# Mixture-of-experts stage: tokens gathered as one f32 product instead of three bfloat16 parts, scratch tiles shared, a twentieth slot in the weight ring

## The chip, the cores and the metric

The kernel runs on one core of a Trainium2 chip. The metric is the device time in microseconds (us) of one execution, lower is better; comparisons use the median of several runs. Five engines work side by side, each through its own queue in order: TensorE (PE in the profile; PEld is its weight load), VectorE (DVE), ScalarE (ACT), GpSimd (POOL) and SyncE (SP), which here issues the DMAs.

## The reference

One layer over 256 tokens of 1024 channels in f32. A modulated norm feeds a Fourier branch and a two-way state-space scan; their gated sum goes through an output projection to the residual `x`. The change lies in the second half:

```python
h2 = rmsnorm(x, norm2_w) * (1.0 + sc2) + sh2
x = x + g2 * moe_ffn(h2, w_router, b_router, w_gate_up, b_gate_up, w_down, b_down)
return rmsnorm(x, final_norm_w)

# moe_ffn, for each of 256 tokens: the 4 best of 32 experts, softmax over the 4 logits
gu = xe @ w_gate_up[e] + b_gate_up[e]            # 1024 -> 2048
gate = minimum(gu[:, :1024], 7.0)
up = clip(gu[:, 1024:], -7.0, 7.0)
act = (up + 1.0) * gate * sigmoid(1.702 * gate)
y = act @ w_down[e] + b_down[e]                  # weighted and added to its token
```

## The kernel before

Everything up to about 560 us (input product, scan, Fourier branch, output projection) is left alone by the change. From there the kernel computes the norm and the routing, and then 32 experts one after the other.

**Weights.** Each expert has 12 chunks of 1 MB: eight of gate/up (one for each 128 of the 1024 input channels) and four of down. `expert_chunk` (L984) issues them on SP's queue, in order, into a ring of tiles: 8 slots `a0` to `a7` in pool `ringA`, 11 slots `b0` to `b10` in `ringB`, 19 in all, taken in the order of the list `RING`. Slots that hold other things in the earlier stage (`xr`, `gn`, `sn2`, `few`, or memory of the earlier stage's tiles under `ringB`) come late in that list. A chunk is issued when its slot's last reader is done and when fewer than 8 are in flight; SP does this in order, so one that waits holds up all behind it. Expert e+1's chunks stand ahead of expert e's work in the program, so about one and a half experts are in the ring.

**The branch of each expert.** An expert's first 64 tokens are always computed. More of them are handled in `overflow(e)`, a chain of branches `tc.If(n_e > 64)` (L1425), `n_e > 96` (L1427) and `n_e > 128` (L1429) which every engine takes, SP too. SP can issue no chunk beyond `If(e)` before PE has come to it, and the slots of e's gate chunks are given back there. `block32` (L1386 to L1408) computes 32 more tokens. In the profiled execution experts 9, 20 and 24 run it once each; I call that a spill.

**Tokens of an expert.** `normed(tb)` (L1097) makes the normed tokens `h2` of one half (128 of 256 tokens) in place, in f32, on DVE. `high_part` (ACT, L1132) and `low_part` (POOL or DVE, L1135) split them into three bfloat16 tiles `h2p[tb][0..2]` whose sum is the f32 value; `h2p` is the first half's tiles and `h2q` the second's. `choose` (L1117 to L1122) picks the four experts, `ranks` numbers the tokens of each expert, and `one_hot` (L1184) writes 0/1 matrices `oh`. `gather_tokens` (L1189) multiplies a token tile with `oh`, so the chosen tokens come out as columns: for each of 8 channel groups k and both halves tb three bfloat16 products, summed in PSUM. One call of `gather` (k4 = 0 or 1) does four of the groups, 24 products. A pair of experts shares one gather of 128 columns; expert e does half of the gather of the next pair (`gather(xe[1 - p2], oh[1 - p2], e % 2)`, for e from 2 to 29), expert 1 does two halves, and `first_gather` does the first pair's. In `block32` the gather has 32 columns and all 16 (k, tb) pairs, 48 products.

**Order within an expert.** PE, DVE, ACT and POOL follow the written order (`manual_schedule`): gate_up (L1277, bias L1287), gather, in even experts `scatter_pair(0)` (L1332), the transposes of `act_T` (L1316), in even experts `scatter_pair(1)`, the branch, down (L1323). Meanwhile DVE and ACT make the activation `ga`, `up` (L1292 to L1297) and `aT`.

Of the kernel before, what the change touches and what calls it, by code (L numbers as in the profile page):

```python
# [9 lines left out]
F32 = mybir.dt.float32  # L10
F32R = mybir.dt.float32r
BF16 = mybir.dt.bfloat16
I32 = mybir.dt.int32
AF = mybir.ActivationFunctionType
# [9 lines left out]
ALPHA = 1.702  # L24
LIMIT = 7.0
CAP = 64
NRA, NRB = 8, 11
PAD = 80

MOD_RATE = {"fourier": 1.0, "gates": 0.5, "z": 0.9}  # L30

# [30 lines left out]
def build(tc, A, out):  # L62
    nc = tc.nc
    V, S, G, T = nc.vector, nc.scalar, nc.gpsimd, nc.tensor
# [20 lines left out]
    ident = ctab[:, C_ID:C_ID + 128]  # L85
# [219 lines left out]
    for k in range(8):  # L305
# [3 lines left out]
        ps = bank("y", 1) if k % 4 == 3 else bank("mm", 3)  # L309
# [119 lines left out]
    for j in range(4):  # L429
        i = j // 2  # L430
        for m, (col, N) in enumerate(FIRST):
# [5 lines left out]
            for k in (2 * j, 2 * j + 1):  # L437
                kw = dict(start=m % 2 == 1, skip_group_check=True) if N == 256 else {}
# [177 lines left out]
    w = next_w()  # L616
    for g in (2, 3):
        with ExitStack() as es:
            if g == 2:
                es.enter_context(tc.issue_after(made.ins))  # L620
            ps = project(w, g, 512)
# [3 lines left out]
    w = next_w()  # L625
# [328 lines left out]
    ms = ExitStack()  # L954
    ringA = pool(ms, "ringA", reuse_waits="tile")
    keepA = pool(ms, "keepA", reuse_waits="tile")
    RING = "a0 a1 a2 a3 b9 b8 b7 b6 b1 b3 b2 b0 b10 b4 b5 a7 a6 a5 a4".split()
    used = [0]

    def tagged(tag, name, shape=(128, 2, 1024)):  # L960
# [106 lines left out]
            project_out(tb, 0, kb)  # L1067


    x2, h2 = acc, xr  # L1070
    h2T = [ap.rearrange("p (k t) -> p k t", k=8) for ap in (sn2[:, 1], gn[:, 0])]
    V.tensor_scalar_mul(gn[:, 0], gn[:, 0], 0.5)
    V.scalar_tensor_tensor(gn[:, 1], sn2[:, 1], 1.0, gn[:, 1], op0=OP.add, op1=OP.mult)
# [7 lines left out]
    def residual(tb, n):  # L1081
        sl = half(n)
        V.tensor_mul(x2[:, tb, sl], xo[tb][n], gn[:, 0, sl])
        V.tensor_add(x2[:, tb, sl], x2[:, tb, sl], xr[:, tb, sl])
        S.activation(xo[tb][n], x2[:, tb, sl], AF.Square, accum_out=ssq2[:, tb, n:n + 1])
        V.tensor_mul(h2[:, tb, sl], x2[:, tb, sl], gn[:, 1, sl])

    def inverse(tb):
        iv = inv2[:, tb:tb + 1]
# [4 lines left out]
    def normed(tb):  # L1094
        iv = inv2[:, tb:tb + 1]
        for n in range(2):
            V.scalar_tensor_tensor(h2[:, tb, half(n)], h2[:, tb, half(n)], iv, sn2[:, 0, half(n)],  # L1097
                                   op0=OP.mult, op1=OP.add)

    def transposed(tb, k2, e):  # L1100
        tp = bank("acc", 8)
        for k in range(4):
            T.transpose(tp[:, k * 128:(k + 1) * 128], h2[:, tb, (k2 * 4 + k) * 128:(k2 * 4 + k + 1) * 128], ident)
        o, i = h2T[tb][:, k2 * 4:k2 * 4 + 4], tp.rearrange("p (k t) -> p k t", k=4)
        if e is S:
            S.activation(o, i, AF.Copy)
        else:
            V.tensor_copy(o, i)
# [12 lines left out]
        V.match_replace(out=mr, in_to_replace=rp, in_values=lgx[:, tb, :], imm_value=3.0e38)  # L1121
        V.tensor_scalar(mask[:, tb, :], mr[:, 0:32], 1.0e38, None, op0=OP.is_gt)  # L1122

    h2p = [[keepA.tile([128, 1024], BF16, name=f"h2p{i}") for i in range(3)]]
    oh = [keepA.tile([128, 2, 128], BF16, name=f"oh{i}") for i in range(2)]
    ohx = keepA.tile([128, 2, 64], BF16, name="ohx")
    woh, woT = (keepA.tile([128, 2, 128], F32, name=n) for n in ("woh", "woT"))
    keepA.tile([128, PAD], F32, name="pad")


    def high_part(tb, i):
        S.activation(h2p[tb][i], h2[:, tb], AF.Copy)  # L1132

    def low_part(tb, i, e):
        e.tensor_sub(h2p[tb][2] if i else h2[:, tb], h2[:, tb], h2p[tb][i])  # L1135

    man = ExitStack()
    ET = mybir.EngineType
# [9 lines left out]
    for kb in range(8):  # L1148
        if kb == 7:
            for k2 in range(2):  # L1150
                transposed(0, k2, S)
        project_out(1, 1, kb)
        if kb == 0:
            residual(0, 1)
            inverse(0)
            normed(0)
            high_part(0, 0)
    low_part(0, 0, G)
    lg = logits(0)
    residual(1, 1)  # L1160
    inverse(1)
    choose(0, lg)
    high_part(0, 1)
    low_part(0, 1, G)
    normed(1)
    us.close()
    ringB = pool(ms, "ringB", reuse_waits="tile")
    for i in range(NRB):
# [2 lines left out]
    work = pool(ms, "work", reuse_waits="tile")  # L1171
    for _ in prefetch:
        pass
    h2p.append([keep.tile([128, 1024], BF16, name=f"h2q{i}") for i in range(3)])
    wt = lambda name, shape, dt=F32: work.tile(list(shape), dt, name=name)
    xe = [wt(f"xe{i}", (128, 8, 128)) for i in range(2)]
    yp = wt("yp", (128, 2, 512))
# [7 lines left out]
                                op0=OP.is_equal)  # L1185

    def gather_tokens(ps, o, k, tb, start, stop, **kw):
        for part in range(3):
            T.matmul(ps, h2p[tb][part][:, k * 128:(k + 1) * 128], o[:, tb, :], start=start and part == 0,  # L1189
                     stop=stop and part == 2, **kw)  # L1190


    pk = bank("acc", 8, shape=(128, 4, 32))
# [14 lines left out]

    for k2 in range(2):
        transposed(1, k2, (V, S)[k2])  # L1210
    high_part(1, 0)
    ranks(0)
    low_part(1, 0, V)
    lg = logits(1)
    first_gather(0, 0)
    choose(1, lg)
    high_part(1, 1)
    low_part(1, 1, G)
    ranks(1)
    for tb in range(2):  # L1220
        T.matmul(pk[:, 2], ones, mask[:, tb], start=tb == 0, stop=tb == 1)
# [34 lines left out]
                V.tensor_add(av, av, tmp)  # L1256


    ga, up, aT = wt("ga", (128, 512)), wt("up", (128, 512)), wt("aT", (128, 4, 128))
    xex = wt("xex", (128, 8, 64))  # L1260
    ssq3 = keep.tile([128, 2, 4], F32, name="ssq3")
    def gather(x, o, k4):

# [48 lines left out]
    def act_T(to):  # L1312
        tp = bank("t", 3, shape=(128, 4, 128))
        upv = up.rearrange("p (f j) -> p f j", j=4)
        for j in range(4):
            T.transpose(tp[:, j, :], upv[:, :, j], ident)  # L1316
        V.tensor_copy(to, tp)

    def down(w, aT):
        pd = bank("dn", 1)  # L1320
        for i, (h, j) in enumerate((h, j) for h in range(2) for j in range(4)):
            for n in range(2):
                T.matmul(pd[n * 64:n * 64 + 64, :], aT[:, j, h * 64:h * 64 + 64],  # L1323
                         w[8 + h * 2 + j // 2][:, j % 2, n * 512:(n + 1) * 512], start=i == 0, stop=i == 7)
        return pd

# [35 lines left out]
    exT = up[:, 0:256].rearrange("p (t c) -> p t c", t=2)  # L1362


    aTx = wt("aTx", (128, 2, 128))
    pos32 = lambda i: ctab[:, C_IOTA + 64 + i * 32:C_IOTA + 96 + i * 32]

    def half32(e, half, w):

        x = xex[:, :, 0:32]  # L1370
        p = bank(*GU[0], shape=(128, 256))
        quarter = lambda ap, q: ap.rearrange("p (h f s c) -> p h s f c", h=2, s=2, c=2)[:, q // 2, q % 2]
        for k in range(8):
            for q in range(4):
                T.matmul(p[q * 32:q * 32 + 32, :], x[:, k, :], quarter(w[k][:, half, :], q),
                         start=k == 0, stop=False, tile_position=(0, q * 32))
        for q in range(4):
            T.matmul(p[q * 32:q * 32 + 32, :], sel[:, e:e + 1].to_broadcast([96, 32]),
                     quarter(bgu[:, half * 1024:half * 1024 + 1024], q), start=False, stop=True,
                     tile_position=(0, q * 32))  # L1380
        return p

    def block32(e, i, w):
        o, x = ohx[:, :, 0:32], xex[:, :, 0:32]
        for tb in range(2):
            V.tensor_scalar(o[:, tb], pos32(i), posm[:, tb, e:e + 1], None, op0=OP.is_equal)  # L1386
        for k4 in range(2):
# [23 lines left out]
    def block64(e, i, w):  # L1411
        one_hot(ohx, (e,), i + 2)
        for k4 in range(2):
            gather(xex, ohx, k4)
        pg, pu = gate_up(e, xex, w)
        gate_act(pg)
        up_act(pu)
        acT = ga.rearrange("p (j c) -> p j c", j=4)
        act_T(acT)
        weights_T(exT, slots_of(i + 2).unsqueeze(1).to_broadcast([128, 2, 64]), (e,))  # L1420
        V.tensor_mul(ga, down(w, acT), g2b)
        scatter(exT, ga)

    def overflow(e, n_e, w):
# [19 lines left out]
    for e in range(NE):  # L1444
# [30 lines left out]
            gather(xe[1 - p2], oh[1 - p2], e % 2)  # L1475
        if e and e % 2 == 0:
            scatter_pair(0)
        act_T(aT)
        if e and e % 2 == 0:
            scatter_pair(1)  # L1480
        if last:
# [3 lines left out]
            for k4 in range(2):  # L1485
                gather(xe[1], oh[1], k4)
        overflow(e, n_e, w)
        pd = down(w, aT)
        if e >= NE - 2:
            V.tensor_mul(yp[:, e % 2], pd, g2b)  # L1490
        else:
# [57 lines left out]
```

## Time and profile before

| | us |
|---|---|
| median of 3 runs | 1601.92 (1598.63 to 1603.74) |
| profiled execution, device time | 1596.67 |
| its span in the trace | 1594.9 |
| PE busy | 1432.5 (90%) |
| DVE, ACT, POOL busy | 660.2, 304.1, 200.9 |
| DMA bytes | 511.75 MB |

The span is the profiled execution's; what lies outside is 1.8 us. Busy shares are means over stages with different limits. An idle gap is put down to the work that ended it: `[0.57 <-DVE up L1297]` behind a row says that its engine sat idle 0.57 us before and was released by that write.

### The profile page before, as it was taken

What the parts mean: (1) busy time and instruction counts of PE and PEld (TensorE: products, weight loads), DVE (VectorE), ACT (ScalarE), POOL (GpSimd) and SP (SyncE); (2) the same over time, 40 slices, a digit from 0 to 9 for tenths busy, and PEclk for the clock granted to TensorE, in tenths of its full rate; (3) what the DMA queues carried; (4) which work ended last, traced back from release to release, by engine and by line L of the source; (5) the groups of instructions that cost most, each with busy time, mean ns of one, the idle gap of its engine ahead of it and who ended that gap; (6) DMA issues with size and microseconds to landing.
All of it is one profiled execution on the core that took longest, in us unless ns stands there. A gap on an engine that the chain in (4) does not pass through costs nothing. (4 is left out here: it accounts for less than half of the span.)

```text
span 1594.9 us, 21869 instructions
## 1 busy us (share of the span) xinstructions
PE 1432.5 (90%) x8684; PEld 806.0 (51%) x8684; DVE 660.2 (41%) x1158; ACT 304.1 (19%) x635; POOL 200.9 (13%) x165
## 2 busy tenths in 40 slices
PE   6998988889999988998988889989888989899897
PEld 4887766678899753433333333433334334343332
DVE  5776887885575743212222222212213123121222
ACT  3446354444555420000000000000000000000001
POOL 0155143332460410000000000000000000000000
PEclk8999999999999978999999999999989999999999
DMA  9625244578769757999999899999997999699993
GB/s 290 215 76 192 87 125 158 151 231 278 274 235 339 268 211 316 384 418 418 419 418 418 351 418 418 418 419 418 418 419 299 418 418 417 257 418 418 418 418 154
DMA packets 121636, 511.75 MB, mean 321 GB/s; under 512 B 13800, under 2 KB 30928, under 8 KB 72448
## 3 DMA queue, kind: packets, MB, share of 16 engines
q1 hardware_dynamic: 121472, 509.56, 81.8%
q8 instruction: 103, 1.69, 0.4%
q14 instruction: 61, 0.50, 0.1%
HBM read 508.33 MB, written 1.20 MB: 319 GB/s over the span
## 5 line engine op out<-in xcount | busy, mean ns | idle before, releaser
L1277 PE MATMUL ps_gu<-wexp,xe 128*64 128x512 f32 x2048 | 462.2, 607 | 6.3 <-DMA wexp<-in_w_gate_up 6.3
L1277 PEld LDWEIGHTS ps_gu<-wexp,xe 128*64 128x64 f32 x2048 | 157.1, 140 | 294.9 <-issue 269.9
L1323 PE MATMUL ps_dn<-wexp,aT 128*64 128x512 f32 x1024 | 234.2, 610 | 32.5 <-DVEq L1425 21.3
L1292 DVE TENSOR_SCALAR ga<-ps_gu 128x512 f32<-128x512 f32 x32 | 22.1, 691 | 437.7 <-issue 405.6
L1323 PEld LDWEIGHTS ps_dn<-wexp,aT 128*64 128x64 f32 x1024 | 85.6, 140 | 169.8 <-issue 120.3
L343 PE MATMUL ps_mm<-hh,wh 128*128 128x256 f32 (+1 forms) x496 | 166.8, 336 | 2.3 <-DVE cv L472 2.3
L345 PE MATMUL ps_mm<-hh,wl 128*128 128x256 f32 (+1 forms) x496 | 163.1, 329 | 0.0
L344 PE MATMUL ps_mm<-hl,wh 128*128 128x256 f32 (+1 forms) x496 | 162.6, 328 | 0.0
L1293 ACT ACTIVATE ga<-ga 128x512 f32<-128x512 f32 x32 | 20.2, 631 | 660.5 <-DVE ga L1292 660.5
L1328 DVE TENSOR_TENSOR yp<-ps_dn,g2b 64x512 f32<-64x512 f32 x60 | 41.3, 689 | 231.1 <-PE ps_dn L1323 230.6
L336 POOL TENSOR_TENSOR wl<-wraw,wh 128x512 fp32r<-128x512 f32 x78 | 105.0, 1349 | 218.7 <-ACT wh L333 164.0
L1502 POOL TENSOR_TENSOR ssq<-ssq,mhalf 128x1 f32<-128x1 f32 x2 | 1.1, 550 | 1013.2 <-DVE ssq L1501 1013.2
L343 PEld LDWEIGHTS ps_mm<-hh,wh 128*128 128x128 f32 x496 | 95.3, 192 | 23.8 <-issue 7.7
L345 PEld LDWEIGHTS ps_mm<-hh,wl 128*128 128x128 f32 x496 | 95.5, 193 | 10.0 <-issue 2.2
L344 PEld LDWEIGHTS ps_mm<-hl,wh 128*128 128x128 f32 x496 | 95.4, 192 | 8.2 <-issue 1.2
L333 ACT ACTIVATE wh<-wraw 128x512 fp32r<-128x512 f32 x132 | 81.1, 627 | 86.3 <-PE ps_mm L344 71.6
L472 DVE SCALAR_TENSOR_TENSOR cv<-ps_mm,par,cv 128x508 f32<-128x508 f32 (+3 forms) x116 | 80.8, 697 | 5.0 <-ACT cv L466 3.2
L336 DVE TENSOR_TENSOR wl<-wraw,wh 128x512 fp32r<-128x512 f32 x54 | 49.8, 924 | 36.3 <-ACT wh L333 35.5
L1334 DVE TENSOR_TENSOR acc<-acc,ps_sc 128x512 f32<-128x512 f32 x76 | 51.5, 685 | 19.0 <-PE ps_sc L1332 17.0
L1332 PE MATMUL ps_sc<-yp,woT 128*128 128x512 f32 x120 | 57.4, 601 | 0.0
L706 ACT ACTIVATE ab<-ab,nacs 128x128 f32<-128x128 f32 x128 | 42.1, 390 | 51.9 <-POOL ab L703 51.7
L1310 ACT ACTIVATE woT<-ps_t 128x256 f32<-128x256 f32 x15 | 5.8, 384 | 237.2 <-PE ps_t L1309 237.2
(373 smaller groups left out, 1809.5 us busy)
## 6 DMA issues: line engine op xcount, KB each, us to landing
wexp<-in_w_gate_up SPq DMA_DIRECT2D x256, 1024.0 KB, 19.9
wexp<-in_w_down SPq DMA_DIRECT2D x127, 1024.0 KB, 19.9
wraw<-in_w_in SPq DMA_DIRECT2D x32, 1024.0 KB, 5.0
wmod<-in_w_mod SPq DMA_DIRECT2D x64, 256.0 KB, 5.3
wmod<-in_w_mod SPq DMA_DIRECT2D x16, 512.0 KB, 8.3
ab<-ad SPq DMA_DIRECT2D x32, 256.0 KB, 3.7
eb<-ad SPq DMA_DIRECT2D x32, 256.0 KB
wssd<-in_w_ssd_out SPq DMA_DIRECT2D x8, 1024.0 KB, 8.6
```

What stands on the lines that cost most here:

```text
L333: S.activation(shp, w, AF.Copy)
L336: e.tensor_sub(low.rearrange("p (k n) -> p k n", n=128), w, shp.bitcast(F32))
L343: T.matmul(ps[:, :N], hi, hh[k][:, :N], start=k == 0 and start, stop=False, **kw)
L344: T.matmul(ps[:, :N], hi, hl[k][:, :N], start=False, stop=False, **kw)
L345: T.matmul(ps[:, :N], low, hh[k][:, :N], start=False, stop=k == 7, **kw)
L472: V.scalar_tensor_tensor(yv[:, :, a], pv[:, :, b], convw(k, blk), yv[:, :, a], op0=OP.mult, op1=OP.add)
L706: S.activation(ab[:, h, :], ab[:, h, :], AF.Exp, bias=nacs[:, c, j0 + h:j0 + h + 1])
L1277: mm = T.matmul(ps[half][h * 64:h * 64 + 64, :], x[:, k, :], w[k][:, half, h * 512:(h + 1) * 512], start=k == 0, stop=False)
L1323: T.matmul(pd[n * 64:n * 64 + 64, :], aT[:, j, h * 64:h * 64 + 64], w[8 + h * 2 + j // 2][:, j % 2, n * 512:(n + 1) * 512], start=i == 0, ...
L1328: V.tensor_mul(y, p[n * 64:n * 64 + 64, :], g2b[n * 64:n * 64 + 64])
L1332: T.matmul(p, lhsT, rhs, start=True, stop=True)
L1334: V.tensor_add(av, av, p)
```

## The change

The normed tokens stay f32: `normed` reads `xr` and writes `h2a` (first half) or `h2b`. The three bfloat16 tiles, `high_part` and `low_part` go, with three ACT casts, three POOL subtractions and one on DVE; `oh`, `ohx` become f32, and `gather_tokens` issues one f32 product for each (k, tb). `aT`, `aTx` and `xex` have no tiles of their own any more: the transposed activation goes into the expert's own, already used token columns `xs`, and the spill's tiles into the upper half of `ga`. The room goes to slot `b11`, which stands behind `b10` in `RING`. `normed(1)` stands behind the ring's allocation in the text. Core of the diff:

```diff
-NRA, NRB = 8, 11
-PAD = 80
+NRA, NRB = 8, 12
+PAD = 16
-    RING = "a0 a1 a2 a3 b9 b8 b7 b6 b1 b3 b2 b0 b10 b4 b5 a7 a6 a5 a4".split()
+    RING = "a0 a1 a2 a3 b9 b8 b7 b6 b1 b3 b2 b0 b10 b11 b4 b5 a7 a6 a5 a4".split()
...
-    x2, h2 = acc, xr
+    x2, hraw = acc, xr
...
     def normed(tb):
         iv = inv2[:, tb:tb + 1]
         for n in range(2):
-            V.scalar_tensor_tensor(h2[:, tb, half(n)], h2[:, tb, half(n)], iv, sn2[:, 0, half(n)],
+            V.scalar_tensor_tensor(h2[tb][:, half(n)], hraw[:, tb, half(n)], iv, sn2[:, 0, half(n)],
                                    op0=OP.mult, op1=OP.add)
...
-    h2p = [[keepA.tile([128, 1024], BF16, name=f"h2p{i}") for i in range(3)]]
-    oh = [keepA.tile([128, 2, 128], BF16, name=f"oh{i}") for i in range(2)]
-    ohx = keepA.tile([128, 2, 64], BF16, name="ohx")
+    h2 = [keepA.tile([128, 1024], F32, name="h2a")]
+    oh = [keepA.tile([128, 2, 128], F32, name=f"oh{i}") for i in range(2)]
+    ohx = keepA.tile([128, 2, 64], F32, name="ohx")
...
-    def high_part(tb, i):
-        S.activation(h2p[tb][i], h2[:, tb], AF.Copy)
-
-    def low_part(tb, i, e):
-        e.tensor_sub(h2p[tb][2] if i else h2[:, tb], h2[:, tb], h2p[tb][i])
...
             normed(0)
-            high_part(0, 0)
-    low_part(0, 0, G)
     lg = logits(0)
     residual(1, 1)
     inverse(1)
     choose(0, lg)
-    high_part(0, 1)
-    low_part(0, 1, G)
-    normed(1)
     us.close()
...
-    h2p.append([keep.tile([128, 1024], BF16, name=f"h2q{i}") for i in range(3)])
+    h2.append(keep.tile([128, 1024], F32, name="h2b"))
+    normed(1)
...
     def gather_tokens(ps, o, k, tb, start, stop, **kw):
-        for part in range(3):
-            T.matmul(ps, h2p[tb][part][:, k * 128:(k + 1) * 128], o[:, tb, :], start=start and part == 0,
-                     stop=stop and part == 2, **kw)
+        T.matmul(ps, h2[tb][:, k * 128:(k + 1) * 128], o[:, tb, :], start=start, stop=stop, **kw)
...
         transposed(1, k2, (V, S)[k2])
-    high_part(1, 0)
     ranks(0)
-    low_part(1, 0, V)
     lg = logits(1)
     first_gather(0, 0)
     choose(1, lg)
-    high_part(1, 1)
-    low_part(1, 1, G)
     ranks(1)
...
-    ga, up, aT = wt("ga", (128, 512)), wt("up", (128, 512)), wt("aT", (128, 4, 128))
-    xex = wt("xex", (128, 8, 64))
+    ga, up = wt("ga", (128, 512)), wt("up", (128, 512))
+    xex = ga.rearrange("p (k c) -> p k c", k=8)
...
-    aTx = wt("aTx", (128, 2, 128))
+    xe32 = ga[:, 256:512].rearrange("p (k c) -> p k c", k=8)
+    aTx = ga[:, 256:512].rearrange("p (c f) -> p c f", c=2)
...
-        act_T(aT)
+        act_T(xs)
...
-        pd = down(w, aT)
+        pd = down(w, xs)
```

How it stands on the engines, at three places. On PE, in expert 2, the last of the eight (k, tb) pairs of the gather (`h2q` the second half's parts, `oh` the one-hots, with buffer numbers) and what follows up to the branch, before:

```order
L1189 LDWEIGHTS h2q_6119
L1189 MATMUL ps_t<-oh_5938,h2q_6119 128x128
L1189 LDWEIGHTS h2q_6120
L1189 MATMUL ps_t<-oh_5938,h2q_6120 128x128
L1189 LDWEIGHTS h2q_6121
L1189 MATMUL ps_t<-oh_5938,h2q_6121 128x128
L1332 MATMUL ps_sc<-yp,woT 128x512 x2
L1316 MATMUL ps_t<-ctab,up 128x128 x4
L1332 MATMUL ps_sc<-yp,woT 128x512 x2
L1425 COMPARE_AND_BRANCH
```

and in the changed kernel the last two pairs:

```order
L1177 MATMUL ps_t<-oh_5936,h2a 128x128
L1177 MATMUL ps_t<-oh_5936,h2b 128x128
L1315 MATMUL ps_sc<-yp,woT 128x512 x2
L1299 MATMUL ps_t<-ctab,up 128x128 x4
L1315 MATMUL ps_sc<-yp,woT 128x512 x2
L1408 COMPARE_AND_BRANCH
```

Three loads and three products have become one product, whose weight load is part of it; the work behind it stands as before.

On POOL, from the end of the output projection (`wol` are its low parts) to the first expert's branch, before:

```order
L1045 TENSOR_TENSOR wol<-wo,woh 128x512 x6
L1092 TENSOR_TENSOR inv_5260<-inv_5260,mhalf 128x1
L1135 TENSOR_TENSOR xr<-xr,h2p_5935 128x1024
L1092 TENSOR_TENSOR inv_5260<-inv_5260,mhalf 128x1
L1135 TENSOR_TENSOR h2p_5937<-xr,h2p_5936 128x1024
L1135 TENSOR_TENSOR h2q_6121<-xr,h2q_6120 128x1024
L1457 TENSOR_LOAD cnt
L1425 COMPARE_AND_BRANCH
```

and in the changed kernel:

```order
L1045 TENSOR_TENSOR wol<-wo,woh 128x512 x6
L1092 TENSOR_TENSOR inv_5260<-inv_5260,mhalf 128x1 x2
L1440 TENSOR_LOAD cnt
L1408 COMPARE_AND_BRANCH
L1410 COMPARE_AND_BRANCH
```

The three subtractions of 128x1024 are gone; DVE keeps its order of `choose(0)`, `normed(1)`, `choose(1)` and loses one subtraction of its own.

On SP, expert 0's last three gate chunks and its first two of down, with the semaphores that each waits for (DMAHW n are earlier DMAs), before:

```order
L984 DMA wexp<-in_w_gate_up 128x2048 [waits DMAHW5_49,PE_49]
L984 DMA wexp<-in_w_gate_up 128x2048 [waits Pool_49]
L984 DMA wexp<-in_w_gate_up 128x2048 [waits DMAHW7_49]
L984 DMA wexp<-in_w_down 128x2048 [waits DMAHW0_49,DVE_49,Pool_49]
L984 DMA wexp<-in_w_down 128x2048 [waits DMAHW1_49,DMAHW2_49,DVE_49,Pool_49]
```

and in the changed kernel:

```order
L984 DMA wexp<-in_w_gate_up 128x2048 [waits DMAHW5_49,PE_49]
L984 DMA wexp<-in_w_gate_up 128x2048 [waits Pool_49]
L984 DMA wexp<-in_w_gate_up 128x2048 [waits DMAHW7_49,PE_49,Pool_49]
L984 DMA wexp<-in_w_down 128x2048 [waits DMAHW1_49,DMAHW0_49,DVE_49]
L984 DMA wexp<-in_w_down 128x2048 [waits DMAHW2_49,DVE_49]
```

The last gate chunk now also waits for PE and POOL: the slots lie 1 KB further on in memory, and `b6` touches a tile of the output projection that is read until its last product (L1062).

## Rows read from the trace of the kernel before

**Rows 1.** Waits of SP's queue: who released it, us in total, times, longest.

```profile
SPq L984 <- PEq L1425: 192.2, 23, 24.1
```

**Rows 2.** PE, timeline (start, us, instructions): gates of experts 2 and 18.

```profile
647.28 13.93 PE L1277 MATMUL ps_gu<-wexp,xe 128*64 128x512 f32 x64
...
1125.41 1.06 PE L1277 MATMUL ps_gu<-wexp,xe 128*64 128x512 f32 x4
...
1143.18 0.60 PE L1287 MATMUL ps_gu<-bgu,sel 96*64 96x512 bf16 x4
```

**Rows 3.** SP, timeline: the last gate chunks of experts 18 and 20.

```profile
1118.02 2.84 SPq L984 DMA_DIRECT2D wexp<-in_w_gate_up  x2
...
1179.82 2.84 SPq L984 DMA_DIRECT2D wexp<-in_w_gate_up  x2
```

**Rows 4.** PE, timeline: end of expert 20's gate (its bias).

```profile
1205.48 0.62 PE L1287 MATMUL ps_gu<-bgu,sel 96*64 96x512 bf16 x4
```

**Rows 5.** PE, timeline: gather of expert 2, first row of eight, and what follows.

```profile
661.58 0.34 PE L1189 MATMUL ps_t<-oh,h2p 128*128 128x128 bf16 x3
...
662.93 1.94 PE L1332 MATMUL ps_sc<-yp,woT 128*128 128x512 f32 x4
```

**Rows 6.** PE, timeline: behind the gather of expert 3.

```profile
694.17 0.75 PE L1316 MATMUL ps_t<-ctab,up 128*128 128x128 f32 x4 [0.58 <-DVE up L1297]
```

**Rows 7.** PE, timeline: two f32 products of 128 columns, two records each.

```profile
334.31 0.39 PE L803 MATMUL ps_t<-cdsd,uT 128*128 128x128 f32 x2
334.54 0.39 PE L804 MATMUL ps_t<-cdsd,od 128*128 128x128 f32 x2
```

**Rows 8.** PE, timeline: gather of expert 9's spill, first row of sixteen, then gate.

```profile
869.01 0.23 PE L1189 MATMUL ps_t<-ohx,h2p 128*128 128x32 bf16 x3 [1.02 <-DVE ohx L1386]
...
870.31 5.35 PE L1375 MATMUL ps_gu<-wexp,xex 128*32 128x256 f32 x64
```

**Rows 9.** PE, timeline: logits of both halves, eight f32 products of 32 columns each.

```profile
561.12 1.97 PE L1113 MATMUL ps_acc<-few,sn 128*128 128x32 f32 x16 [0.16 <-ACT sn L1106]
...
570.09 3.60 PE L1113 MATMUL ps_acc<-few,gn 128*128 128x32 f32 x16
```

**Rows 10.** Windows: length, busy PE, PEld, DVE, ACT, POOL, granted clock, DMA share, GB/s.

```profile
566.50:571.00 4.50, 2.92 (x15) 2.96 (x15) 3.39 (x7) 0.95 (x2) 0.74 (x1) 0.50 0.97 388
...
870.20:873.40 3.20, 3.20 (x39) 1.52 (x39) 0.29 (x1) 0.00 (x0) 0.00 (x0) 0.50 1.02 420
```

**Rows 11.** DVE and POOL, timelines: residual, choose of both halves, and first subtraction.

```profile
555.57 0.69 DVE L1084 TENSOR_TENSOR acc<-acc,xr 128x512 f32<-128x512 f32 x1
...
561.73 1.61 DVE L1084 TENSOR_TENSOR acc<-acc,xr 128x512 f32<-128x512 f32 x1
...
565.34 1.94 DVE L1122 TENSOR_SCALAR few<-few 128x32 f32<-128x32 f32 x1
...
574.19 1.98 DVE L1120 COPY few<-few 128x4 f32<-128x4 f32 x1
...
576.50 0.18 DVE L1122 TENSOR_SCALAR few<-few 128x32 f32<-128x32 f32 x1
...
560.66 2.13 POOL L1135 TENSOR_TENSOR xr<-xr,h2p 128x1024 f32<-128x1024 f32 x1 [2.62 <-ACT h2p L1132]
```

**Rows 12.** PE, timeline: end of the first gather and gate of expert 0.

```profile
580.21 2.77 PE L1189 MATMUL ps_acc<-oh,h2q 128*128 128x128 bf16 x24
582.91 14.18 PE L1277 MATMUL ps_gu<-wexp,xe 128*64 128x512 f32 x64
```

**Rows 13.** PE, timeline: expert 1's first gather row; downs of 1, 15, 19.

```profile
635.41 0.53 PE L1189 MATMUL ps_t<-oh,h2p 128*128 128x128 bf16 x3
...
640.39 7.09 PE L1323 MATMUL ps_dn<-wexp,aT 128*64 128x512 f32 x32 [0.89 <-DVEq L1425]
...
1061.59 8.61 PE L1323 MATMUL ps_dn<-wexp,aT 128*64 128x512 f32 x32 [1.78 <-PEq L1425]
...
1182.19 9.74 PE L1323 MATMUL ps_dn<-wexp,aT 128*64 128x512 f32 x32 [3.43 <-PEq L1425]
```

More of the change, by code (lines that the diff above doesn't have):

```diff
@@ L1085, in residual @@
         S.activation(xo[tb][n], x2[:, tb, sl], AF.Square, accum_out=ssq2[:, tb, n:n + 1])
-        V.tensor_mul(h2[:, tb, sl], x2[:, tb, sl], gn[:, 1, sl])
+        V.tensor_mul(hraw[:, tb, sl], x2[:, tb, sl], gn[:, 1, sl])
     def inverse(tb):
@@ L1102, in transposed @@
         for k in range(4):
-            T.transpose(tp[:, k * 128:(k + 1) * 128], h2[:, tb, (k2 * 4 + k) * 128:(k2 * 4 + k + 1) * 128], ident)
+            T.transpose(tp[:, k * 128:(k + 1) * 128], h2[tb][:, (k2 * 4 + k) * 128:(k2 * 4 + k + 1) * 128], ident)
         o, i = h2T[tb][:, k2 * 4:k2 * 4 + 4], tp.rearrange("p (k t) -> p k t", k=4)
@@ L1316, in act_T @@
             T.transpose(tp[:, j, :], upv[:, :, j], ident)
-        V.tensor_copy(to, tp)
+        V.tensor_copy(to, tp.rearrange("p j (h c) -> p (j h) c", h=2))
     def down(w, aT):
@@ L1322, in down @@
             for n in range(2):
-                T.matmul(pd[n * 64:n * 64 + 64, :], aT[:, j, h * 64:h * 64 + 64],
+                T.matmul(pd[n * 64:n * 64 + 64, :], aT[:, 2 * j + h, :],
                          w[8 + h * 2 + j // 2][:, j % 2, n * 512:(n + 1) * 512], start=i == 0, stop=i == 7)
@@ L1362, in build @@
     exT = up[:, 0:256].rearrange("p (t c) -> p t c", t=2)
-    aTx = wt("aTx", (128, 2, 128))
+    xe32 = ga[:, 256:512].rearrange("p (k c) -> p k c", k=8)
+    aTx = ga[:, 256:512].rearrange("p (c f) -> p c f", c=2)
     pos32 = lambda i: ctab[:, C_IOTA + 64 + i * 32:C_IOTA + 96 + i * 32]
     def half32(e, half, w):
-        x = xex[:, :, 0:32]
+        x = xe32
         p = bank(*GU[0], shape=(128, 256))
@@ L1383, in block32 @@
     def block32(e, i, w):
-        o, x = ohx[:, :, 0:32], xex[:, :, 0:32]
+        o, x = ohx[:, :, 0:32], xe32
         for tb in range(2):
@@ L1417, in block64 @@
         up_act(pu)
-        acT = ga.rearrange("p (j c) -> p j c", j=4)
-        act_T(acT)
+        act_T(xex)
         weights_T(exT, slots_of(i + 2).unsqueeze(1).to_broadcast([128, 2, 64]), (e,))
-        V.tensor_mul(ga, down(w, acT), g2b)
+        V.tensor_mul(ga, down(w, xex), g2b)
         scatter(exT, ga)
```

## The prediction

> **What bounds the kernel now.** The page gives PE 90% of the span, but that mean hides two regimes, so I read the expert stage by its waits, first SP's, then PE's. SP's longest single kind of wait is for PE's branch at L1425 [rows 1]: the chunks of the next experts stand behind that branch, so the weight stream stops until PE gets there and then restarts. While it runs, one chunk of 1 MB is issued every 2.5 us (two issues over 2.84 us, each 0.33 [rows 3]), so an expert's twelve take 30 us, a little more than PE needs for an expert. PE starts each run of the stream with weights in hand and uses them up. A gate that never waits takes 13.9 us; expert 18's takes 17.8, from 1125.41 to its bias at 1143.18, 3.9 of them waiting for chunks [rows 2]. Expert 8 does the same on a run that began at expert 1's branch, expert 18 on one that began behind the spill of expert 9. Expert 20 is close: its last gate chunk was issued at 1182.33 and used at about 1203.7 (the bias, less an eighth of 13.9), 21.4 us later [rows 3, 4], where expert 18's, waited for, took 20.9. So it had 0.5 us to spare. Behind the spills of experts 20 and 24 the stream is ahead of PE, and no wait of PE for a chunk is left; from there each us of PE work goes straight to the end.
>
> So the end is read at five points: expert 1's branch, the stream to experts 8 and 9, the spill of 9, the stream to expert 20, and all PE work behind it.
>
> **Price of a product.** A (k, tb) pair costs three bfloat16 products now. At 128 columns expert 2's gather runs from 661.58 to 662.93, 1.35 us for 24 [rows 5], 0.168 a pair. An f32 product of 128 columns is two records, and the next product starts 0.23 us after it [rows 7]; I take 0.224, two of 0.112. Eight pairs: 1.79, so +0.45 us for an expert's gather. At 32 columns the spill's sixteen rows of three lie between 869.01 and the next line at 870.31 [rows 8]: 1.2 us for 16 pairs. The logits are f32 products of 32 columns, eight of them in 16 records: 1.97 us in one place, 3.60 in the other [rows 9], where the granted clock is 0.50, the lower of the two levels [rows 10]; 0.112 and 0.213 us a record. Sixteen pairs are 32 records: 3.6 us at the upper level, 6.8 at the lower. Less 1.2, a spill pays +2.4 to +5.6.
>
> A rule of the Trainium skill speaks on this price: its page "FP8 and Floating Point Precision", section "TensorE Precision Notes", has true f32 as four passes through the array. As an estimate from that page, four passes of 32 columns at 2.4 GHz are 0.053 us, sixteen pairs 0.85, and a spill would gain 0.35. The logits' rows speak against it (0.224 for a product of 32 columns, as much as for 128), and the page "TensorE: Matmul & The Clock Gate", section "Weight-path perf modes — Fast Weight Load (FWL) and DoubleRow", would explain that: the fast weight load is not used with FP32.
>
> **Part by part.**
>
> *Start.* Three DVE operations stand on the path from the last output product to expert 0, and each ran beside a POOL subtraction of 2.1 us: the residual add 1.61 us against 0.69 earlier, L1122 1.94 against 0.18, L1120 (a smaller copy) 1.98 [rows 11]. The subtractions go, so these should fall to their usual length: 0.9 + 1.7 + 1.8 = 4.4 us saved. The ACT casts and the DVE subtraction lay beside PE's logits, nothing for them. Against that, two of the three first gathers are on the path at the lower clock: 24 products take 2.77 us there [rows 12], 2.6 without the tail; eight f32 pairs take 16 x 0.213 = 3.4, and the half-sized one adds half as much again: +1.3. Net -3.1. Bounds: if the clock does not fall any more in the shorter wait, up to -6; if only part of the stretch goes, -1.5.
>
> *Expert 1* makes two halves of a gather, sixteen rows from 635.41 (the first at 0.53, so part of it at the lower clock) to some 0.9 before the down at 640.39 [rows 13], 4.0 us. In f32: 32 records, 3.6 to 6.8, so -0.4 to +2.8; I take the middle, +1.2.
>
> So expert 1's branch comes at -1.9.
>
> *The first chunks.* `b6` now waits for the last output product, just ahead of the logits at 561.12 [rows 9], and all chunks behind it in SP's queue with it. Twelve chunks of 2.5 us land by about 593. Expert 0's products begin near 580 and run 14 us [rows 12], and its branch comes behind the activation, later than 595; SP would stop at that branch anyway. Cost nothing; without that cover up to 22 us of lost issuing would show.
>
> *The twentieth slot.* At each stop of the stream one chunk more is already in the ring. That brings the stream 2.5 us forward on each run that PE catches up with: the one to experts 8 and 9, and the one from 9 to 20. Twice -2.5.
>
> *Gathers of experts 2 to 29.* Behind an even expert's gather PE goes straight on with the scatter [rows 5]: +0.45. Behind an odd one PE waits 0.58 us for `up` [rows 6], which covers 0.45; if `up` came earlier it would cost as much again. Ahead of expert 20 the even ones only eat into waits for chunks; from 20 on there are five: +2.25.
>
> *Spills.* Three times. PE idles 1.02 us just ahead of the gather, and in expert 9 the clock is down to 0.50 behind it [rows 8, 10]. With half of the records at each level (16 x 0.112 + 16 x 0.213 = 5.2, less 1.2) a spill pays +4.0. I take that, between 2.4 and 5.6, because a gather three times as long, with only 32 columns in flight, is likelier to fall into the lower level than the present one. All three count: that of 9 stops the stream, those of 20 and 24 are behind the last wait.
>
> *Shared tiles.* The transposed activation, the spill's tokens and its transposes overwrite data whose readers stand earlier on PE in the same expert; nobody waits longer. Nothing; 0.1 us for an expert if a DVE copy had to wait. The one-hots are off the path except `ohx`, 0.1 us either way.
>
> *Branches.* In experts 15 and 19 PE waited 1.78 and 3.43 us at the branch, instead of 0.89, and the down behind it ran 8.61 and 9.74 instead of 7.09 [rows 13]: 7.6 us in all. In the trace a fetch of PE's program falls right there. Each expert's program is shorter by about 140 PE instructions, so these places move; by counting, to experts 14 and 17, ahead of the wait at 18, and none behind 20. Then PE is at expert 20 ahead of its chunks again and the stream sets the time: its -2.5 and the 0.5 that were to spare. With the waits left where they are, PE would be last by 1.0 and the sum that much higher.
>
> **Sum.** -1.9 (expert 1) - 2.5 (slot) + 4.0 (spill of 9) - 2.5 (slot) - 0.5 (spare at 20) + 2.25 (gathers) + 8.0 (spills of 20 and 24) = +6.8 us. The profiled execution's 1596.67 becomes 1603.5; against the median, 1601.92, it is 1608.7. I give the latter, since the profiled one was faster than all three timed.
>
> **Rivals.**
>
> *The clock stays up.* Spills at 2.4 each: 3 x 1.6 less, +2.0, 1603.9. For it: two of the three spills have no fall in the trace. Against: the gather becomes three times as long.
>
> *The clock stays down* through all spill gathers, 5.6 each: +4.8, so +11.6, 1613.5.
>
> *The slot does not act*, because the eight in flight and not the slots hold the stream: both -2.5 gone, +11.8, 1613.7. Against: behind each branch several chunks are issued at once, so it is slots that came free.
>
> *The other side: f32 products as cheap as their columns.* If the loads of f32 weights hide behind the stream when sixteen products stand in a row, a spill costs -0.35 to 0 and expert 1 and the start none: -4.4 (start) - 5.0 (slot) - 0.5, +2.25 at most from the even gathers, so -7.7, 1594.2. It decides from a pair of 0.1 us downwards; the even experts alone cannot turn the sign. For it: no f32 gather is in the trace. Against: logits and L803, 0.224 both. A part of its chance is a start at -6 with spills at 2.4, about -1. The four passes of the Trainium skill's page "FP8 and Floating Point Precision", section "TensorE Precision Notes", taken alone, would give this case.
>
> **How the numbers follow.** Forecast 0.41, clock up 0.21, clock down 0.12, slot idle 0.09, the other side 0.17. About 0.3%, 4.8 us, is what a measurement can tell from no change. The forecast is slower by more in three quarters of its cases (0.31), clock down and slot idle in all (0.21): 0.52. Same: the rest of the forecast, clock up, and a little of the other side, 0.32. Faster: 0.16. The range leaves out the far end of the other side and of the clock-down case: 1599 to 1616.
>
> **What would show it.** After: L1135 gone and L1122, L1120 near 0.2; expert 0's gate 3 us earlier; 32 records in a spill's gather over 3.6 to 6.8 us; even gathers 1.8; expert 18 waiting 1 us instead of 3.9; expert 20 waiting some 4; no wait for chunks behind it. It is wrong if a gather row in f32 takes under 0.2 a pair, if DVE's three operations stay long, or if PE waits for chunks behind expert 24.

## The result

The changed kernel is slower: 1616.26 us (median of 14 runs, 1606.21 to 1622.80) against 1602.06 us, ratio 1.0083 with a 95% interval of 1.0062 to 1.0103. That is 10 to 16.5 us, 13.3 at the middle, where the prediction had +6.8 and 1608.7. The direction was right, the size was off by a factor of two, and the median lies a quarter of a microsecond above the range. One run of experiment e6 further down, at 1929.92 us with a granted clock of 0.737, is in the slow state and left out of its numbers.

The two profiled executions are 23.6 us apart in their spans (1618.5 and 1594.9), because the one before was a short one of its kind and the one after a long one. So the traces are compared piece by piece, not by their ends. First what the prediction had listed. DVE at the start, timeline of the changed kernel (start, us, instructions; answers to [rows 11]):

```profile
564.71 0.69 DVE L1084 TENSOR_TENSOR acc<-acc,xr 128x512 f32<-128x512 f32 x1
...
567.40 0.18 DVE L1122 TENSOR_SCALAR few<-few 128x32 f32<-128x32 f32 x1
...
574.01 0.17 DVE L1120 COPY few<-few 128x4 f32<-128x4 f32 x1
```

The three stretched operations are short again: 0.69, 0.18 and 0.17 us where 1.61, 1.94 and 1.98 stood. PE's first gathers and the gate of expert 0 in the changed kernel (answers to [rows 12]):

```profile
579.09 3.62 PE L1177 MATMUL ps_acc<-oh,h2b 128*128 128x128 f32 x16
582.64 14.06 PE L1260 MATMUL ps_gu<-wexp,xe 128*64 128x512 f32 x64
```

The gather is dearer, 3.62 us for 2.77. From the end of the last output product the gate comes 18.7 us later, before it was 21.95: 3.3 us saved, forecast 3.1. The gathers, PE in the changed kernel: expert 2 (answers to [rows 5]), then the spills of experts 9 and 20 (answers to [rows 8]):

```profile
665.41 0.49 PE L1177 MATMUL ps_t<-oh,h2a 128*128 128x128 f32 x2
...
667.30 1.88 PE L1315 MATMUL ps_sc<-yp,woT 128*128 128x512 f32 x4
...
879.45 0.38 PE L1177 MATMUL ps_t<-ohx,h2a 128*128 128x32 f32 x2 [1.02 <-DVE ohx L1370]
...
883.11 5.48 PE L1359 MATMUL ps_gu<-wexp,ga 128*32 128x256 f32 x61
...
1223.03 0.41 PE L1177 MATMUL ps_t<-ohx,h2a 128*128 128x32 f32 x2 [0.93 <-DVE ohx L1370]
...
1225.05 0.61 PE L1177 MATMUL ps_t<-ohx,h2a 128*128 128x32 f32 x2
1225.48 0.61 PE L1177 MATMUL ps_t<-ohx,h2b 128*128 128x32 f32 x2
...
1228.58 4.70 PE L1359 MATMUL ps_gu<-wexp,ga 128*32 128x256 f32 x56
```

An expert's gather takes 1.89 us for 1.35, forecast 1.79. A spill's takes 3.66 us at the upper clock level (expert 9) and 5.55 where the clock falls inside it (expert 20: a pair every 0.22 us, then every 0.43). From PE's branch to the down, the spills of experts 9, 20 and 24 take 26.7, 28.7 and 29.4 us, before 24.0, 24.8 and 23.2: +12.7, forecast +12.0. PE waits for chunks in experts 18 and 20, whose gates are 2.2 and 4.9 us longer than one that never waits, forecast 1 and 4, and not behind 20.

So far the sum holds. What it did not have is in the list of PE's waits in the changed kernel (who released it, us in total, times, longest), and in the downs of experts 4 and 7 (`issue` marks idle time in which PE waited for nothing that the profile shows):

```profile
PE ps_dn L1306 <- issue: 4.7, 3, 2.5
PE ps_dn L1306 <- PEq L1408: 1.8, 2, 1.6
PE ps_t L1177 <- issue: 0.8, 1, 0.8
```

```profile
729.80 2.33 PE L1306 MATMUL ps_dn<-wexp,xe 128*64 128x512 f32 x9 [0.88 <-DVEq L1408]
733.70 3.65 PE L1306 MATMUL ps_dn<-wexp,xe 128*64 128x512 f32 x16 [1.57 <-issue]
...
817.43 1.94 PE L1306 MATMUL ps_dn<-wexp,xe 128*64 128x512 f32 x8 [0.89 <-DVEq L1408]
821.86 7.03 PE L1306 MATMUL ps_dn<-wexp,xe 128*64 128x512 f32 x24 [2.49 <-issue]
```

Eight or nine records into a down that waits for no data PE stands still for 1.6 and 2.5 us, and the clock falls in expert 7's (granted clock 0.85 over it), so that this down takes 11.5 us instead of 7.1; expert 29's has a shorter gap of 0.6, and so has the gather in the spill of expert 24, 0.8 (the third line). The kernel before had one such gap of 1.1 us, in expert 22, beside its two waits at the branches of 15 and 19 [rows 13]. In the changed kernel those two branches are clean. Of the two places that the prediction counted out, expert 17 waits 1.55 us at its branch instead of 0.89; at 14 the branch itself takes 1.5 us instead of 0.4, but the down behind it starts no later.

What fits these gaps is a wait of PE for its own program. It is read by DMA in pieces of 16 KB, as queue q8 of the changed kernel's page has them (packets, MB, share of the 16 engines), and then what the queues moved in the stretch 729.8 to 731.2 (one row) and in the stretch 731.2 to 732.4 (two rows):

```profile
q8 instruction: 107, 1.75, 0.4%
```

```profile
q1 hardware_dynamic: 79, 0.58, 100.1%
...
q1 hardware_dynamic: 68, 0.48, 97.9%
q8 instruction: 1, 0.02, 5.7%
```

In the first stretch the engines move weights only; in the second, 3.8 us behind the branch at 727.5, one piece of program comes in, and PE goes on after it. Such a fetch is no sign of a stop by itself: one begins 3.4 to 3.9 us behind most branches in all these traces, also where PE does not stand still. What the gaps have in common is their end: in all 27 of them (four here, one in the kernel before, the others in e2, e3 and e5 below) PE's next product starts 2.3 to 2.9 us after the fetch began.

Up to the first expert, 29 pieces are read for about 7,500 records of PE in the trace, loads and products, so a piece holds about 260 instructions; I count with 256 (an f32 product of two records, with a load each, counts four). Counted like that, the program behind the branch of expert 4 begins at 0.70 of a piece, that of 7 and that of 29 at 0.72. PE stands still 24 to 43 records later, at 0.80 to 0.89 by the same count and not at 1.00, so my count carries the distances between places, and not where a piece ends. As I read it, PE jumps close to the end of a piece and is through with the rest before the next has come.

### The profile page after: what moved, and what is told of

Same layout as the page of the kernel before. It is cut to its first block, busy times and chain, and to the rows that moved or that the text cites. A ratio compares the mean times of both kernels' runs of the same rounds, so it can differ in the third digit from the quotient of the medians.

```text
span 1618.5 us, 21244 instructions
## 1 busy us (share of the span) xinstructions
PE 1466.9 (91%) x8380; PEld 836.4 (52%) x8380; DVE 659.4 (41%) x1157; ACT 300.3 (19%) x631; POOL 192.9 (12%) x162
## 5 line engine op out<-in xcount | busy, mean ns | idle before, releaser
L1306 PE MATMUL ps_dn<-wexp,xe 128*64 128x512 f32 x1024 | 234.5, 608 | 33.1 <-DVEq L1408 21.3
L1306 PEld LDWEIGHTS ps_dn<-wexp,xe 128*64 128x64 f32 x1024 | 86.1, 140 | 170.3 <-issue 121.6
```

Of the source, the lines that this page charges most:

```text
L1306: T.matmul(pd[n * 64:n * 64 + 64, :], aT[:, 2 * j + h, :], w[8 + h * 2 + j // 2][:, j % 2, n * 512:(n + 1) * 512], start=i == 0, stop=i == 7)
```

## The experiments

**Theory A:** where each expert's branch, and the program behind it, falls in these pieces costs time, and the change moved it. **Theory B:** the f32 gathers are dearer than the sum had them. **Theory C:** the clock falls more often by chance. Differences between two kernels are taken from their ratios, times 1602, unless a single time is named. Each experiment is the changed kernel or the one before with unused code added, in numbers that put the branches where its expectation says; e5, e6 and e7 are e1 and e9 is e8 with one edit more, shown without that code, and with numbers of their own where the edit moves the branches. The labels e1 to e9 follow the order below. The code sits in the branch for more than 128 tokens, which no expert takes:

```diff
+    FILL = [74, 18, 38, 43, 38, 44, ...]
+
+    def unused_code(n):
+        pd = bank("dn", 1)
+        for _ in range(n // 2):
+            T.matmul(pd[:, 0:128], ident, ident, start=True, stop=True)
+        for _ in range(n % 2):
+            T.transpose(pd[:, 0:128], ident, ident)
...
                     for i in range(2):
                         block64(e, i, w)
+                    if FILL[e]:
+                        unused_code(FILL[e])
```

**The changed kernel with every expert at the same place of a piece.**

> Changed kernel with 18 to 74 products or transposes added to code that is never run (the branch for more than 128 tokens), so many for each expert that every expert's program behind its branch begins at the same place of a 16 KB piece, 0.35 of it, and the branch itself falls near 0.32 to 0.37. Work done is the same. Theory A (the place of the branch in the pieces of PE's program costs time: in the changed kernel PE stands still in the downs of experts 4, 7 and 29 for want of the next piece, 1.6, 2.5 and about 0.7 us, and the clock falls there): no idle time put down to issue in the downs, no wait of 1.5 us or more at a branch, and 6 to 8 us less than the changed kernel, ratio to before about 1.004. Theory B (the f32 gathers are dearer than the sum had them, above all in spills): the same as the changed kernel, 1.008. Theory C (the clock falls by chance in the gaps of an expert, more often in the changed kernel): the same within 2 us.

Measured: 1605.65 us, ratio to before 1.0035 (1.0017 to 1.0052); the changed kernel stands at 1.0083. In the list of PE's waits no gap put down to issue is left, and one short wait at a branch:

```profile
PE ps_dn L1306 <- PEq L1417: 0.3, 1, 0.3
```

Not one executed instruction of data work differs, and by the ratios 7.7 us are gone; the two intervals do not overlap. Theory A.

**The kernel before, treated in the same way.**

> Kernel before with unused code added in the same way, program behind every branch at 0.30 of a piece, work the same. Theory A: the waits of 1.8 and 3.4 us at the branches of experts 15 and 19 and the 1.1 us in the down of 22 go; but expert 20 then waits for its chunks, so only 1 to 2.5 us less than before, ratio 0.9985 to 0.9995. With e1 that leaves about 9 us for the change itself, against 6.8 in the prediction. Theories B and C: 1.000.

A miss: 1607.83 us, 1.0026 (1.0011 to 1.0041), slower. The waits of experts 15, 19 and 22 are gone as expected, but the place I had chosen makes new ones. PE in the spill of expert 9 of this kernel, and the waits list:

```profile
877.24 1.92 PE L1375 MATMUL ps_gu<-wexp,xex 128*32 128x256 f32 x11
881.82 1.51 PE L1375 MATMUL ps_gu<-wexp,xex 128*32 128x256 f32 x12 [2.67 <-issue]
```

```profile
PE ps_gu L1375 <- issue: 5.6, 3, 2.7
```

A spill goes straight on behind the branch, and here PE stops 121 to 125 records behind it, 2.7, 1.5 and 1.4 us, in all three spills. By the count that is 0.80 to 0.87 of a piece, where the changed kernel stops too. This is theory A again, at another place than I had looked.

**The changed kernel with every expert at the bad place.**

> Changed kernel with the unused code chosen so that every expert's program behind its branch begins at 0.70 of a piece, where experts 4, 7 and 29 of the changed kernel stand. Theory A: nearly every down has a gap of 1 to 2.5 us put down to issue soon after its start, 30 to 60 us in all, and the kernel is slower than the changed one by 25 us or more. Theories B and C: no gap of this kind beyond the three there, same time as the changed kernel.

A single run: 1633.65 us, beside 1602 before. The waits list, and expert 3's down:

```profile
PE ps_dn L1306 <- issue: 16.1, 16, 2.2
PE ps_t L1177 <- issue: 3.8, 2, 2.0
```

```profile
701.00 2.33 PE L1306 MATMUL ps_dn<-wexp,xe 128*64 128x512 f32 x9 [0.89 <-DMA wexp<-in_w_gate_up]
705.56 4.94 PE L1306 MATMUL ps_dn<-wexp,xe 128*64 128x512 f32 x22 [2.22 <-issue]
```

Sixteen downs have the gap, not nearly all, and the stops add up to 20 us, less than the 30 I had as a minimum; the time is 17 us above the changed kernel and not 25 or more, 28 above e1. The place makes the gap. The gaps lie in experts up to 19, and they shrink: 23 to 30 records behind the branch and up to 2.2 us long in experts 2 to 7, 31 to 42 records and 0.2 to 0.8 us in experts 11 to 19. So the places that I had made equal still drift, and the product behind a gap always starts 5.9 to 6.4 us behind the branch in experts 2 to 19. That late experts go without a gap because PE now gets to the end of the piece after that time would follow, but no run shows it.

**The kernel before, at a place without stops.**

> Kernel before with unused code once more, now so that the program behind each branch begins at 0.95 of a piece and the branch falls near 0.0, where the spills of the kernel before (branches at 0.50, 0.04 and 0.95) stood without a gap. In e2 the branches at 0.33 to 0.38 put the end of a piece into the gate of each spill, 2.7 us of standing still three times. Theory A: those three go, nothing comes in their place, and the time is 1 to 3 us below the kernel before, ratio 0.998 to 1.000. The change without any stop for program pieces is then e1 against this run, 1.004 to 1.005. If it stays at e2's 1.0026, something other than those stops makes the added code dear.

1596.27 us, 0.9971 (0.9958 to 0.9984). No gap put down to issue is left, but a short wait at the branch of expert 29:

```profile
PE ps_dn L1323 <- PEq L1434: 1.5, 2, 1.2
```

So the stops of the kernel before were worth 4.6 us (2.6 to 6.7 by the interval), more than the 1 to 3 expected, and the change all but without stops is e1 against e4: 1.0035/0.9971 = 1.0064, 10.3 us (about 7 to 14 by the two intervals).

**The spill's gather halved.**

> e1 with the gather of block32 taking its tokens from the first half alone: 8 f32 products instead of 16 in each of three spills; tokens of the second half are left out of the spill's columns. Theory B (spill gathers are the larger part of the loss): 16 records fewer, 1.8 us at the upper clock level and 3.4 at the lower, three times, so 5.5 to 10 us below e1, ratio to before 0.997 to 1.000. If the spill's gather is hidden or small: within 2 us of e1.

```diff
         for k4 in range(2):
-            gather(x, o, k4)
+            ps = bank("t", 3, shape=(128, 4, 32))
+            for k in range(4):
+                gather_tokens(ps[:, k, :], o, k4 * 4 + k, 0, True, True)
+            V.tensor_copy(x[:, k4 * 4:k4 * 4 + 4, :], ps)
```

1598.59 us, 0.9977 (0.9960 to 0.9995): 9.3 us below e1, from 24 products of 32 columns fewer, since three spills leave out eight each. The whole gather of expert 9's spill in this kernel, sixteen records:

```profile
867.43 2.12 PE L1177 MATMUL ps_t<-ohx,h2a 128*128 128x32 f32 x16 [1.02 <-DVE ohx L1370]
```

It is as the expectation says of where the cost lies, and at the size that the sum gave it. From PE's branch to the down the spills of experts 9, 20 and 24 are 1.6, 3.5 and 3.5 us shorter than in e1, 8.6 together; in the first a gap of 1.2 us put down to issue is new. So the gathers are not dearer than the sum had them, as theory B had it at first.

**Nineteen slots.**

> e1 without slot b11, all else the same. Prediction's sum: a chunk less at both stops of the stream, 5 us above e1, ratio 1.0065. From e1's trace, where expert 8 does not wait for chunks and experts 18 and 20 do: only the run from expert 9 to 20 counts, 2.5 us above e1, ratio 1.005. If the slot does not act: the same as e1, 1.0035.

```diff
-NRA, NRB = 8, 12
+NRA, NRB = 8, 11
-    RING = "a0 a1 a2 a3 b9 b8 b7 b6 b1 b3 b2 b0 b10 b11 b4 b5 a7 a6 a5 a4".split()
+    RING = "a0 a1 a2 a3 b9 b8 b7 b6 b1 b3 b2 b0 b10 b4 b5 a7 a6 a5 a4".split()
```

1608.81 us (median of six runs), 1.0051 (1.0032 to 1.0070): 2.6 us above e1 by the ratios. The two intervals overlap, so the size rests on the traces. Gate of expert 8 on PE, in e4, in e1 and here:

```profile
819.38 3.83 PE L1277 MATMUL ps_gu<-wexp,xe 128*64 128x512 f32 x16
823.77 1.94 PE L1277 MATMUL ps_gu<-wexp,xe 128*64 128x512 f32 x8 [0.56 <-DMA wexp<-in_w_gate_up]
...
838.01 0.60 PE L1287 MATMUL ps_gu<-bgu,sel 96*64 96x512 bf16 x4
```

```profile
821.79 13.93 PE L1260 MATMUL ps_gu<-wexp,xe 128*64 128x512 f32 x64
```

```profile
817.88 13.93 PE L1260 MATMUL ps_gu<-wexp,xe 128*64 128x512 f32 x64
```

In e4 expert 8 waits for chunks: its gate takes 18.6 us up to the bias, where one that never waits takes 13.8. In e1 it does not wait, and with a slot less it does not either. From the first product of expert 1's down to the bias of expert 8's gate it is 193.5 us in e4, 193.2 in e1 and 193.4 here: in e1 and e6 PE itself needs as long as the stream with 19 slots, so the chunk that the slot brings earlier is not what anyone waits for. What makes PE slower there are the gathers of experts 2, 4 and 6, 0.45 us each, and more than twice as much the clock. The gate of expert 3 in e4 and in e1, at a granted clock of 1.00 and 0.91:

```profile
681.91 13.95 PE L1277 MATMUL ps_gu<-wexp,xe 128*64 128x512 f32 x64
```

```profile
680.28 15.33 PE L1260 MATMUL ps_gu<-wexp,xe 128*64 128x512 f32 x64
```

The gate of expert 7 is 1.7 us longer in the same way. Both are long in the changed kernel, e1, e5, e6, e7 and e8, and neither is in the kernel before and e4; but in e2, which has the old gathers, both are as well, and in e3 only that of 7, so what lowers the clock there I did not settle.

At experts 18 and 20 PE waits in all three (the gates are 4.4 and 4.9 us longer than one that never waits in e6, 3.1 and 3.3 in e1). First product of expert 9's down and bias of expert 20's gate, in e4, in e1 and in e6:

```profile
895.60 4.94 PE L1323 MATMUL ps_dn<-wexp,aT 128*64 128x512 f32 x22 [0.88 <-DVEq L1436]
...
1209.02 0.60 PE L1287 MATMUL ps_gu<-bgu,sel 96*64 96x512 bf16 x4
```

```profile
898.91 7.09 PE L1306 MATMUL ps_dn<-wexp,xe 128*64 128x512 f32 x32 [0.89 <-DVEq L1419]
...
1210.47 0.60 PE L1270 MATMUL ps_gu<-bgu,sel 96*64 96x512 bf16 x4
```

```profile
891.61 7.09 PE L1306 MATMUL ps_dn<-wexp,xe 128*64 128x512 f32 x32 [0.89 <-DVEq L1419]
...
1205.04 0.60 PE L1270 MATMUL ps_gu<-bgu,sel 96*64 96x512 bf16 x4
```

That run takes 313.4 us with 19 slots, in e4 as in e6, and 311.6 with 20: 1.9 us for the slot here, and 2.3 in e8. The slot counts at one stop, not two.

**The POOL subtractions put back.**

> e1 with three POOL subtractions of 128x1024 put back where the kernel before has them; they write tokens that nobody reads any more. Prediction's step: DVE's residual add, L1122 and L1120 are stretched again by 0.9 + 1.7 + 1.8 us, expert 0's gate comes 4.4 us later and the end as well, ratio 1.006. If the start's saving does not reach the end: the same as e1.

```diff
             normed(0)
+    G.tensor_sub(hraw[:, 0], hraw[:, 0], h2[0])
     lg = logits(0)
...
     choose(0, lg)
+    G.tensor_sub(hraw[:, 0], hraw[:, 0], h2[0])
...
     choose(1, lg)
+    G.tensor_sub(hraw[:, 1], hraw[:, 1], h2[1])
     ranks(1)
```

1613.95 us, 1.0066 (1.0043 to 1.0089), 5.0 above e1 with few runs. DVE and POOL in this kernel:

```profile
575.01 2.12 DVE L1122 TENSOR_SCALAR few<-few 128x32 f32<-128x32 f32 x1
...
584.05 0.17 DVE L1120 COPY few<-few 128x4 f32<-128x4 f32 x1
...
574.76 2.34 POOL L1155 TENSOR_TENSOR xr<-xr,h2a 128x1024 f32<-128x1024 f32 x1
```

The second subtraction stretches L1122 from 0.18 to 2.12 us. The other two no longer meet anything long, since they start at other moments than in the kernel before, and expert 0's gate comes only 2.1 us later than in e1. The mechanism is there; the full 4.4 was not reproduced, and what the timing adds above 2.1 is within its interval. The clock differs too: 0.961 on average in these four runs, 0.966 in e1's.

**The changed kernel at e4's place.**

> Changed kernel with unused code that puts the program behind each branch at 0.02 of a piece, the branch near 0.0, the place of e4. If the stops for program pieces are all that the place does (theory A), the same as e1 within 2 us, 1.002 to 1.005, and against e4 the change costs 8 to 11 us. If e1 stood at a lucky place, 3 us or more above e1.

1609.63 us, ratio 1.0036 (1.0019 to 1.0053), as e1, and 10.4 us against e4. So e1 did not stand at a lucky place.

**Two bfloat16 parts.**

> Shared tiles and the twentieth slot as in the changed kernel, but tokens as two bfloat16 parts (high and low, the third part is left out) in the room of the f32 tiles, two products for each pair; program behind the branch at 0.02 of a piece. It is to keep the slot and the cheap loads of bfloat16 weights. From the traces: a pair costs 0.11 us at 128 columns and 0.05 at 32; against e4 an expert's gather 0.45 less, a spill 0.4 less, the start 2 to 4 us less (two POOL subtractions instead of three, two thirds of the first gathers), one slot's 2.5 us: 6 to 11 us below e4, ratio to before 0.990 to 0.994. If f32 was not what made the changed kernel slower, it stays near e1, 1.003.

```diff
-    h2 = [keepA.tile([128, 1024], F32, name="h2a")]
+    h2 = [[keepA.tile([128, 1024], BF16, name=f"h2a{i}") for i in range(2)]]
...
+    def parts(tb):
+        S.activation(h2[tb][0], hraw[:, tb], AF.Copy)
+        G.tensor_sub(h2[tb][1], hraw[:, tb], h2[tb][0])
...
-        T.matmul(ps, h2[tb][:, k * 128:(k + 1) * 128], o[:, tb, :], start=start, stop=stop, **kw)
+        for part in range(2):
+            T.matmul(ps, h2[tb][part][:, k * 128:(k + 1) * 128], o[:, tb, :], start=start and part == 0,
+                     stop=stop and part == 1, **kw)
```

1584.54 us, 0.9882 (0.9865 to 0.9899), the fastest of all: 18.9 us below the kernel before and 14 below e4, more than the 6 to 11 expected. PE in expert 2 and in the spill of expert 9:

```profile
659.29 0.28 PE L1183 MATMUL ps_t<-oh,h2a 128*128 128x128 bf16 x2
...
660.20 1.94 PE L1323 MATMUL ps_sc<-yp,woT 128*128 128x512 f32 x4
...
864.02 0.20 PE L1183 MATMUL ps_t<-ohx,h2a 128*128 128x32 bf16 x2 [1.02 <-DVE ohx L1378]
...
865.06 5.43 PE L1367 MATMUL ps_gu<-wexp,ga 128*32 128x256 f32 x64
```

A pair costs 0.11 us at 128 columns (0.91 for eight) and 0.05 at 32, where the f32 product takes 0.22 at both. With two bfloat16 parts in the room of the f32 tiles, the rest of the change (slot, shared tiles, one POOL subtraction for each half) pays, taken together; how much each brings was not measured. One part shows in the trace: here the slot counts at both stops. From expert 1's down to the bias of expert 8's gate it is 191.2 us, 2.3 less than in e4, and from expert 9's down to that of expert 20's 310.9, 2.5 less. The kernel does less than the other two, since the third part is left out.

## Why the prediction was off

*What bounds the kernel* was right but for one of its five points: in the changed kernel PE waits for chunks at 18 and 20 and not behind, but not at 8 either. The gathers of even experts are exposed, those of odd ones are not: the branch comes 2.46 us behind the end of the gate in expert 3 of both kernels. One reading was off: the branch is not SP's longest kind of wait; by the same list SP waits longer in total for chunks to land (289.9 us for gate chunks alone, in 146 waits of 3.1 at most). Nothing in the sum hangs on it.

*Price of a product, start, spills* were right. Start -3.3 (forecast -3.1), gather +0.5 (+0.45), spills +12.7 in the trace (+12.0), 0.8 of it the gap in the spill of 24; in e1 against e4 the spills are +10.3. The clock stood between the two levels, as taken: up through the gather of 9, down in half of that of 20.

*The Trainium skill's four passes* ("FP8 and Floating Point Precision", section "TensorE Precision Notes"), taken as columns alone, would have a spill's gather shorter than before; the trace has 0.224 us for a product of 32 columns, the same as for 128. The measurement decides against that reading.

*Expert 1* came out at +4.2 from the first product of expert 0's down to that of its own (39.2 us before, 43.4 after), not +1.2. Its gather is 0.8 us longer (638.40 to about 643.2); the rest is the down of expert 0, 10.04 instead of 8.41 us, and a gate of 15.65 instead of 13.95, with the clock lower in the changed kernel's trace (0.70 for 0.84, 0.89 for 1.00). In e5 and e6 that stretch is 38.7 and 38.8 us, shorter than before, and in e1 42.6. So most of the difference comes and goes with the clock; whether the change makes it likelier, these traces do not show.

*The twentieth slot* was counted twice, -5.0; it counts once, -1.9 by e6's trace and -2.6 by its ratio. The step that failed is the run to experts 8 and 9: it took PE to arrive there ahead of the stream, as it does before. With the dearer gathers and the lower clock in the gates of experts 3 and 7 PE needs as long as the stream with 19 slots, the stops in the downs of 4 and 7 add 5 us more, and the earlier chunk saves nothing. That is +2.5 against the sum. In e9, with cheap gathers, the slot did count twice.

*Branches* were put at -1.0, and this is the step that failed most. The prediction saw that PE's program is read in pieces and that the places would move, counted where the branches fall, and was right that 15 and 19 come free and that 17 waits instead. It looked only at stops at a branch. PE also stops a few products behind the jump, by 2.5, 1.6 and 0.6 us in the downs of three experts, and once, by 0.8, in a spill. Together the stops of the changed kernel cost 7.7 us (1.0083 to 1.0035), and those of the kernel before 4.6 (1 to 0.9971): net +3.1 where -1.0 stood.

By these, 6.8 + 2.5 (slot) + 4.1 (stops) = 13.4, and 13.3 were measured. The agreement to a tenth is chance, since each of the ratios is known to some 3 us. Theory C stays open for a part. The granted clock of an execution moves by 0.008 among the changed kernel's runs, and their times by 16 us with it. A straight line through each kernel's runs gives, at a clock of 0.966, 1613 us for the changed kernel, 1607 and 1608 for e1 and e8, 1600 for the kernel before and 1599 for e4: as an estimate from these, at equal clock the stops of the changed kernel cost 6 us and the change without stops 9, so that one or two us of each go with the clock. What of that the gathers cause, I did not separate. Of the rivals none came about as a whole: the clock neither stayed up nor down, the slot acts at one of its two stops, and no f32 product was as cheap as its columns.

## What to carry to other kernels

Before a change to a kernel with long branches is judged, its program's place should be taken out of the comparison: code that never runs, added so that each branch and its target keep clear of such places, moved the two kernels by 4.6 and 7.7 us, where the change itself is 10.3; at a place badly chosen (e2) it made the kernel before slower by 4.2. A buffer that lets a stream run ahead is worth its time only at the stops where the consumer arrives first, and an edit that slows the consumer takes that away at the same time. For small products, count the weight loads by type: two or three bfloat16 products can be cheaper than one in f32.

## What the runs showed of the hardware

In these traces a piece of PE's program that comes late stops PE for 0.2 to 2.7 us, with weights moving at full rate beside it; PE goes on 2.3 to 2.9 us after the fetch of the piece began. It happens at a branch when a fetch falls there (3.4 us in expert 19 of the kernel before, where it begins 1.4 us behind the branch), in the first products behind a jump that lands at 0.70 to 0.72 of a piece by my count (2.5 us in the changed kernel), and behind a branch that is not taken (2.7 us in e2).

The product behind an f32 product of 32 columns starts 0.22 us later at the upper clock level and 0.43 us later at the lower, like one of 128 columns. Two bfloat16 products of 32 columns take 0.05 us. The Trainium skill's "TensorE: Matmul & The Clock Gate", section "Weight-path perf modes — Fast Weight Load (FWL) and DoubleRow", has the fast load only for types other than FP32; these rows agree, though none shows a load by itself.
